# Eight gate tiles of a hybrid attention layer are computed in the recurrent stretch and applied later

## The chip, the cores and the metric

The kernel runs on one core of a Trainium2 chip. The metric is the device time of one execution in microseconds; the median of three runs is 1376.31 us (1373.77 to 1378.28). The engines are TensorE (PE, its weight loads PEld), VectorE (DVE), ScalarE (ACT), GpSimd (POOL) and SyncE (SP, which issues the DMAs here).

## The reference, cut to what matters

One layer works on 256 latent tokens, with 256 context tokens ahead of them, at width 2048. One input projection feeds two branches: an RWKV-7 recurrence (16 heads of 64) and a gated linear attention, GLA (4 heads, key 128, value 256). Each branch's output is normed and multiplied by a SiLU gate, projected to 2048, weighted by a sigmoid gate, summed and projected again.

```python
p = h @ w_in          # columns: r k v | z_a | lora_w lora_a | q_b k_b v_b | z_b | lora_g | g_a g_b
...
y_a = (y_a + bonus) * silu(z_a)
ob  = o_b * rsqrt(mean(o_b * o_b, -1) + EPS) * b_norm_g
y_b = ob.reshape(bsz, t, B_WIDTH) * silu(z_b)
mixed = sigmoid(g_a) * (y_a @ w_a) + sigmoid(g_b) * (y_b @ w_b)
return mixed @ w_out
```

Only the latent tokens need z_a, z_b, g_a and g_b. z_b has 1024 columns: eight tiles of 128 columns by 256 tokens, two for each GLA head.

## The kernel before

Weights come from HBM in fp32. A "raw" tile of 512 KB is loaded by a DMA on SP's queue (three are held, `NRAW`), and `splitter` takes it apart in two halves: ScalarE casts the half to a rounded fp32 (wH), VectorE subtracts to get the rest (wL), 128x512 elements each, up to five halves ahead (`NSPLIT`). `stream` then issues the dense matmuls, three for each block of 128 rows (high by high, high by low, low by high), into a PSUM tile "acc" (or "pv" for the values). A tile of 128 output columns over 2048 rows is 16 x 3 = 48 matmuls, of 256 columns for latent tokens alone and of 512 for all tokens (K and V). The jobs stand in one list in a fixed order (`jobs`, `pick`); a job with a `take` that says no is skipped if it has `skip`.

The instruction order of all engines is made at build time by a planner, `Issue`. Work is written as tracks (generators with a priority); `Issue.run` keeps a modelled time of each engine and picks the next step: the ready one with the lowest priority number within a short window. The dense stream has priority 99, the last. It goes ahead of other TensorE work only if 1200 ns of small work have been issued since the last dense block (`since`), or if `cooling` says that the count of matmul columns is too low. `cooling` counts columns in fixed slots of modelled time. `small` sums the modelled TensorE time of the small work.

The stages:

- the opening, up to 145 us: modulation, norm, the first seven K tiles;
- the GLA stretch (A), up to about 580 us: for each head its q, k and v columns, two K/V tiles for the recurrence (each followed by a 3x3 convolution on VectorE, `conv_ops`), and two z_b tiles (`add_zb`). `sz_track` turns a z_b tile into a gate (tanh on ScalarE, a multiply on VectorE); `gla_track` transposes the head's normed output, multiplies it by the norm's gain and the gate on VectorE, and stores it to `yb` in DRAM;
- the recurrent stretch (B), up to about 1172 us: eight pairs of heads. For each pair `fe_track` makes features, `ab_track`, `gg_track` the matrices of each chunk, `inv_track` inverts triangular blocks with 60 dependent GpSimd operations on M and tm (the "solve") and some transposes on VectorE (Lin), and `sc_track` runs the scan of 8 steps. The dense jobs r (`rc_track`), z_a (`sz_track`) and the 32 tiles of the merge gates g_a, g_b (`tg_track`, stored to DRAM) are filler. The gate jobs are let in by `pace`: job n when n <= 17 + 32 x small / 230e3;
- the merge (C): `y_track` splits the GLA branch's output, loaded from `yb` into the unused half of mB, then come w_b, w_a and w_out.

S_sz counts the two buffers of the "sz" ring, S_tg those of the "tg" ring. "C" is set in DONE when the last pair's matrices and features are made; the w_b jobs wait for it.

Of the kernel before, what the change touches and what calls it, by code (L numbers as in the profile page):

```python
# [7 lines left out]
F32 = mybir.dt.float32  # L8
# [4 lines left out]
OP = mybir.AluOpType  # L13
# [4 lines left out]
P = 128  # L18
# [6 lines left out]
class Op:  # L25


    __slots__ = ("key", "name", "call", "out", "ins", "cost", "table", "acc", "pe")

    def __init__(self, key, name, call, out, ins, func, acc, psum):  # L30
# [8 lines left out]
        if key == "pe":  # L39
# [3 lines left out]
            if name == "transpose":  # L43
# [4 lines left out]
                       n * (2 if two else 1) * ins[0].shape[0] / 128)  # L48
            c = self.pe[0] * max(self.pe[1:3])
# [27 lines left out]
class Issue:  # L77
# [10 lines left out]
    TICK, COLUMNS = 10240 / 3, 3060  # L88

    def __init__(self, ps, groups):  # L90
# [9 lines left out]
        self.corners, self.ticks = [], {}  # L100

# [37 lines left out]
    def cooling(self):  # L139

        t = self.t["pe"]
        k = int(t // self.TICK)
        rate = (2.4 if self.warm() else 1.2) * 0.6
        return 3100 - self.ticks.get(k, 0) > ((k + 1) * self.TICK - t) * rate

    def emit(self, op):
        r = op.call()
        s = max(self.t[op.key], self.start([op]) + (1220 if op.key == "dma" else 0))
        if op.key == "pe":
# [12 lines left out]
            for _ in range(n):  # L162
# [3 lines left out]
                self.ticks[int(e // self.TICK)] = self.ticks.get(int(e // self.TICK), 0) + cols  # L166
            s = e - op.cost
# [87 lines left out]
    def run(self, done):  # L255
        while not done():
# [9 lines left out]
            if best is None:  # L266
# [8 lines left out]
                if tr[6] == "pe" and best[0] != 99 and 0.6 and self.cooling():  # L275
                    best = next((x for w, x in c if x[0] == 99 and w <= w0 + 150), best)
# [54 lines left out]
def hybrid_layer(tc, a, out):  # L331
    nc = tc.nc
    es = ExitStack()
    with es:
# [197 lines left out]
        PACE0, WB = 17, 230e3  # L532
# [213 lines left out]
        yb = dp.tile([P, 8, 256], F32, name="yb")  # L746
        kv = [[dp.tile([P, 512], F32, name=f"kv{i}_{j}") for j in range(2)] for i in range(8)]
# [42 lines left out]

        def sz_track(acc, key):

            if key[0] == "b":
                yield S_sz.has()
                S_sz.n -= 1
# [43 lines left out]
        def gla_track(h, gp):  # L839
# [106 lines left out]
            for j in range(2):  # L946
                yield lambda: ("b", 2 * h + j) in szs
                pT = yield Claim("gg", [P, 2, P], "pT", *ons)
                yield [PE.transpose(pT[:, tt, :], ons[tt][:, j * P:j * P + P], ident) for tt in range(2)]
                sz = szs.pop(("b", 2 * h + j))  # L950
                yield DV.scalar_tensor_tensor(sz, pT.rearrange("p a b -> p (a b)"), bnh[:, j:j + 1], sz,
                                              op0=OP.mult, op1=OP.mult)
                rel(pT)
                yield DM.dma_start(yb[:, 2 * h + j, :], sz)
# [516 lines left out]
        def add_zb(i):  # L1471
            add_cm(w_in, C_ZB + P * i, "l", CTX, 12, lambda acc: sz_track(acc, ("b", i)))

# [24 lines left out]
        for h in range(4):  # L1498
            for x in rest[:2]:
                add_kv(*x)  # L1500
            add_zb(2 * h)
            add_zb(2 * h + 1)
# [21 lines left out]
        def pace(n):  # L1524
            return lambda: "C" in DONE or n <= PACE0 + 32 * (iss.small - state.get("b0", iss.small)) / WB

        for n in range(32):
# [295 lines left out]
```

## Time and profile before

| | |
|---|---|
| median of 3 runs | 1376.31 us |
| the profiled execution | 1373.94 us |
| its span, first to last instruction | 1372.0 us |
| mean granted TensorE clock | 0.977 of 2.4 GHz |
| TensorE, VectorE, ScalarE, GpSimd busy | 93%, 70%, 52%, 40% |

The busy shares are averages over the stages named above, which have different limits. A busy TensorE is not one at its peak: matmuls are pipelined and their ends are modelled, so one that stands alone counts with its whole latency, while 256-column matmuls in a row follow each other every 0.12 us or so though each is listed with 0.28 us. The chain that ended last tells for each stage which work the next work waited for. Granted clock means the share of 2.4 GHz that TensorE was given in the stretch; there are two levels, 1.2 and 2.4 GHz.

### The profile page before, as it was taken

What the parts mean: (1) busy time and instruction counts of PE and PEld (TensorE: products, weight loads), DVE (VectorE), ACT (ScalarE), POOL (GpSimd) and SP (SyncE); (2) the same over time, 40 slices, a digit from 0 to 9 for tenths busy, and PEclk for the clock granted to TensorE, in tenths of its full rate; (3) what the DMA queues carried; (4) which work ended last, traced back from release to release, by engine and by line L of the source; (5) the groups of instructions that cost most, each with busy time, mean ns of one, the idle gap of its engine ahead of it and who ended that gap; (6) DMA issues with size and microseconds to landing.
All of it is one profiled execution on the core that took longest, in us unless ns stands there. A gap on an engine that the chain in (4) does not pass through costs nothing.

```text
span 1372.0 us, 29669 instructions
## 1 busy us (share of the span) xinstructions
PE 1273.9 (93%) x11479; PEld 1068.6 (78%) x11479; DVE 965.8 (70%) x2031; ACT 717.3 (52%) x1449; POOL 547.8 (40%) x684
## 2 busy tenths in 40 slices
PE   5999989999999999999889999798888999999997
PEld 3555579788788897998777778677777888999877
DVE  4433496875955747767887988797869765667656
ACT  5322244443434444486587577677666656445444
POOL 0000475776560000006798629854947560000002
PEclk9999999999999999999999999899989999999999
DMA  9999465465462533566633344234333545688564
GB/s 347 354 334 305 131 205 173 131 178 162 150 181 78 142 99 102 161 183 164 162 84 87 91 121 111 68 90 113 86 80 99 136 112 149 197 246 262 184 226 144
DMA packets 311185, 220.45 MB, mean 161 GB/s; under 512 B 37354, under 2 KB 286724, under 8 KB 310532
## 3 DMA queue, kind: packets, MB, share of 16 engines
q1 hardware_dynamic: 311044, 218.55, 54.9%
q8 instruction: 90, 1.47, 0.5%
q14 instruction: 51, 0.42, 0.1%
HBM read 199.76 MB, written 12.46 MB: 155 GB/s over the span
## 4 chain that ended last, share of the span: by engine, by line
PE 54%; DVE 17%; POOL 13%; ACT 6%; DMA 5%; issue 5%; SPq 0%; DVEq 0%; ACTq 0%; POOLq 0%
PE acc L304 33%; POOL M L304 6%; POOL tm L304 6%; PE pv L304 6%; DVE wL L304 5%; PE pg L304 3%; DMA raw<-in_w_out_dram 2%; ACT Lin L304 2%; DVE kvo L304 1%; PE pS L304 1%; ACT wH L304 1%; PE pout L304 1%; DVE Lin L304 1%; DVE UV L304 1%; PE pU L304 1%
## 5 line engine op out<-in xcount | busy, mean ns | idle before, releaser
L304 DVE TENSOR_TENSOR wL<-raw,wH 128x512 fp32r<-128x512 f32 x484 | 374.5, 781 | 173.9 <-ACT wH L304 168.0
L304 ACT CAST wH<-raw 128x512 fp32r<-128x512 f32 x484 | 294.6, 615 | 338.9 <-PE acc L304 213.9
L304 PE MATMUL acc<-lH,wH 128*128 128x256 f32 x896 | 286.2, 319 | 0.5 <-ACT tg L304 0.5
L304 PE MATMUL acc<-lL,wH 128*128 128x256 f32 x896 | 257.5, 287 | 0.0
L304 PE MATMUL acc<-lH,wL 128*128 128x256 f32 x896 | 257.0, 287 | 0.1
L304 POOL TENSOR_TENSOR tm<-M 64x30 f32<-64x30 f32 (+14 forms) x240 | 162.7, 678 | 85.8 <-DVE M L304 67.5
L304 PEld LDWEIGHTS acc<-lH,wH 128*128 128x128 f32 x896 | 174.9, 195 | 21.5 <-issue 4.7
L304 POOL TENSOR_TENSOR M<-M,tm 64x30 f32<-64x30 f32 (+14 forms) x240 | 173.4, 722 | 18.7
L304 PEld LDWEIGHTS acc<-lL,wH 128*128 128x128 f32 x896 | 175.6, 196 | 3.1 <-issue 1.9
L304 PEld LDWEIGHTS acc<-lH,wL 128*128 128x128 f32 x896 | 175.4, 196 | 0.3 <-DVE wL L304 0.3
L304 PE MATMUL acc<-hH,wH 128*128 128x512 f32 (+1 forms) x416 | 168.5, 405 | 1.3 <-ACT lo L304 1.3
L304 PE MATMUL acc<-hH,wL 128*128 128x512 f32 (+1 forms) x416 | 157.3, 378 | 0.0
L304 PE MATMUL acc<-hL,wH 128*128 128x512 f32 (+1 forms) x416 | 156.5, 376 | 0.1
L304 PEld LDWEIGHTS acc<-hH,wH 128*128 128x128 f32 x416 | 78.6, 189 | 38.3 <-issue 22.9
L304 POOL TENSOR_TENSOR xs<-yg,fg 128x512 f32<-128x512 f32 (+1 forms) x10 | 13.5, 1365 | 229.8 <-DVE yg L304 229.8
L304 POOL TENSOR_TENSOR gw<-gw,csl 128x512 f32<-128x512 f32 x60 | 73.3, 1222 | 64.6 <-DMA gw<-in_w_mod_dram 64.4
L304 PEld LDWEIGHTS acc<-hH,wL 128*128 128x128 f32 x416 | 78.4, 188 | 15.4 <-DVE wL L304 0.4
L304 POOL TENSOR_TENSOR ga<-ga,gw 128x512 f32<-128x512 f32 x60 | 86.9, 1448 | 4.2
L304 PEld LDWEIGHTS acc<-hL,wH 128*128 128x128 f32 x416 | 78.8, 189 | 10.6 <-DVE hL L304 0.4
L304 PE MATMUL acc<-yH,wH 128*128 128x256 f32 x256 | 72.4, 283 | 1.6 <-DVE mt L304 1.3
L304 PE MATMUL acc<-yL,wH 128*128 128x256 f32 x256 | 72.0, 281 | 0.0
L304 PE MATMUL acc<-yH,wL 128*128 128x256 f32 x256 | 72.0, 281 | 0.0
(318 smaller groups left out, 2621.5 us busy)
## 6 DMA issues: line engine op xcount, KB each, us to landing
raw<-in_w_in_dram SPq DMA_DIRECT2D x174, 512.0 KB, 4.0
wm<-in_w_mod_dram SPq DMA_DIRECT2D x64, 512.0 KB, 6.7
gw<-in_w_mod_dram SPq DMA_DIRECT2D x64, 256.0 KB, 4.1
raw<-in_w_out_dram SPq DMA_DIRECT2D x32, 512.0 KB, 4.6
raw<-in_w_b_dram SPq DMA_DIRECT2D x16, 512.0 KB, 4.0
raw<-in_w_a_dram SPq DMA_DIRECT2D x16, 512.0 KB, 4.3
kv<-kvo SPq DMA_DIRECT2D x16, 256.0 KB, 3.7
tg<-tg SPq DMA_DIRECT2D x32, 128.0 KB, 2.9
```

Of the source, the lines that this page charges most:

```text
L304: op = Op("dma" if name == "dma_start" else self.key, name, lambda: f(*a, **k), aps[0], aps[1:], func, k.get("accum_out"), any(x.tensor.na ...
```

## The change

The eight z_b jobs leave the GLA stretch and stand ahead of the merge gates in the recurrent stretch, under the same pace, whose start goes from 17 to 25 and whose slope from 32 to 40. Their gates go to DRAM (`zs`) through the "tg" ring. A head's GLA output is only scaled by the norm's gain, now on ScalarE, and stored ungated; `y_track` loads the gates beside it and multiplies (VectorE) before the split. `cooling` counts columns over the last 2500 ns of modelled time in place of fixed slots, with small matmuls weighted down. The tiles of the triangular solve are closed once "gi", "vdone" and "bv" of the last pair are there, before it was "gi" alone.

```diff
+            self.flow = n * (1.0 if min(m, ins[0].shape[0]) > 64 else 0.75 if min(m, ins[0].shape[0]) > 32 else 0.5)
...
+    SPAN, NEED = 2500.0, 3600
...
     def cooling(self):
 
         t = self.t["pe"]
-        k = int(t // self.TICK)
-        rate = (2.4 if self.warm() else 1.2) * 0.6
-        return 3100 - self.ticks.get(k, 0) > ((k + 1) * self.TICK - t) * rate
+        while self.past and self.past[0][0] < t - self.SPAN:
+            self.flow -= self.past.popleft()[1]
+        return self.flow < self.NEED
...
+                self.past.append((e, op.flow))
+                self.flow += op.flow
...
-                if tr[6] == "pe" and best[0] != 99 and 0.6 and self.cooling():
+                if tr[6] == "pe" and best[0] != 99 and self.cooling():
...
-        PACE0, WB = 17, 230e3
+        PACE0, NPACE, WB = 25, 40, 230e3
...
+        zs = [dp.tile([P, 256], F32, name=f"zs{i}") for i in range(8)]
...
+        def zs_track(acc, i):
+
+            yield S_tg.has()
+            S_tg.n -= 1
+            sz = pools["com"].tile([P, 256], F32, name="zs", tag="tg", bufs=2)
+            yield AC.activation(sz, acc, AF.Tanh, scale=0.5)
+            yield DV.scalar_tensor_tensor(sz, sz, 1.0, acc, op0=OP.add, op1=OP.mult)
+            rel(acc)
+            yield DM.dma_start(zs[i], sz)
+            S_tg.n += 1
+            DONE.add(("zs", i))
...
             for j in range(2):
-                yield lambda: ("b", 2 * h + j) in szs
+                yield S_sz.has()
+                S_sz.n -= 1
                 pT = yield Claim("gg", [P, 2, P], "pT", *ons)
                 yield [PE.transpose(pT[:, tt, :], ons[tt][:, j * P:j * P + P], ident) for tt in range(2)]
-                sz = szs.pop(("b", 2 * h + j))
-                yield DV.scalar_tensor_tensor(sz, pT.rearrange("p a b -> p (a b)"), bnh[:, j:j + 1], sz,
-                                              op0=OP.mult, op1=OP.mult)
+                ob = pools["com"].tile([P, 256], F32, name="ob", tag="sz", bufs=2)
+                yield AC.activation(ob, pT.rearrange("p a b -> p (a b)"), AF.Copy, scale=bnh[:, j:j + 1])
                 rel(pT)
-                yield DM.dma_start(yb[:, 2 * h + j, :], sz)
+                yield DM.dma_start(yb[:, 2 * h + j, :], ob)
...
-            add_zb(2 * h)
-            add_zb(2 * h + 1)
...
         def pace(n):
-            return lambda: "C" in DONE or n <= PACE0 + 32 * (iss.small - state.get("b0", iss.small)) / WB
-
+            return lambda: "C" in DONE or n <= PACE0 + NPACE * (iss.small - state.get("b0", iss.small)) / WB
+
+        for n in range(8):
+            add_cm(w_in, C_ZB + P * n, "l", CTX, 12, lambda acc, n=n: zs_track(acc, n), take=pace(n), skip=True)
         for n in range(32):
             add_cm(w_in, (C_GA, C_GB)[n % 2] + P * (n // 2), "l", CTX, 12, lambda acc, n=n: tg_track(acc, n // 2, n % 2),
-                   take=pace(n), skip=True)
+                   take=pace(n + 8), skip=True)
...
         def y_track():
             for k in range(0, 8, 2):
+                yield lambda: ("zs", k) in DONE and ("zs", k + 1) in DONE
+                z = mg["mB"][:, k:k + 2, :]
+                for x in range(2):
+                    yield DM.dma_start(z[:, x, :], zs[k + x])
+                yield DV.tensor_tensor(land[:, k:k + 2, :], land[:, k:k + 2, :], z, op=OP.mult)
                 yield from y_split(1, k, 2, land[:, k:k + 2, :])
...
-        iss.run(lambda: ("gi", 7) in DONE)
+        iss.run(lambda: all((x, 7) in DONE for x in ("gi", "vdone", "bv")))
```

## Rows read from the trace of the kernel before

**Rows 1.** Busy time, share of the span and instructions of each engine (the page).
```profile
PE 1273.9 (93%) x11479; PEld 1068.6 (78%) x11479; DVE 965.8 (70%) x2031; ACT 717.3 (52%) x1449; POOL 547.8 (40%) x684
```

**Rows 2.** Busy time of each engine by stage: stretch, its length, engines, clock, DMA.
```profile
core 0: us, PE busy (x) PEld busy (x) DVE busy (x) ACT busy (x) POOL busy (x), PEclk, DMA share, GB/s
145.00:400.00 255.00, 239.92 (x1483) 198.94 (x1483) 193.63 (x353) 102.46 (x194) 165.94 (x134) 0.99 0.56 165
400.00:580.00 180.00, 179.27 (x1214) 157.17 (x1213) 109.69 (x266) 75.10 (x153) 11.73 (x12) 1.00 0.43 119
625.00:680.00 55.00, 48.37 (x453) 45.55 (x453) 46.62 (x69) 31.53 (x53) 46.91 (x66) 0.91 0.62 159
680.00:1060.00 380.00, 341.23 (x4350) 286.72 (x4344) 315.86 (x674) 268.54 (x572) 264.16 (x381) 0.96 0.37 94
```

**Rows 3.** The chain's shares by line, in 145 to 580 and in 625 to 1172.
```profile
by line: PE acc L304 43.6%; PE pv L304 17.7%; DVE wL L304 4.9%; DVE kvo L304 4.1%; PE pS L304 4.0%; issue 3.4%; DVE ro_t L304 2.3%; PE po L304 1.9%; PE plg L304 1.7%; DMA wg<-in_w_in_dram 1.2%; PE pk L304 1.2%; DMA gw<-in_w_mod_dram 1.0%; D
by line: POOL M L304 16.2%; PE acc L304 15.1%; POOL tm L304 14.4%; issue 7.2%; ACT Lin L304 4.3%; DVE wL L304 3.6%; DVE Lin L304 2.5%; DVE UV L304 2.3%; PE pU L304 2.2%; ACT Z L304 2.2%; PE p L304 2.1%; PE pSs L304 1.9%; PE pY L304 1.8%; DV
```

**Rows 4.** Tile acc by stretch: length, PE, PEld, DVE, ACT busy (count), clock, DMA.
```profile
580.00:1172.00 592.00, 332.78 (x2134) 281.42 (x2133) 24.34 (x59) 17.25 (x44) 0.96 0.44 114
680.00:1060.00 380.00, 185.51 (x1119) 150.81 (x1119) 18.67 (x44) 9.57 (x24) 0.96 0.37 94
1121.00:1172.00 51.00, 36.00 (x247) 30.70 (x246) 0.00 (x0) 1.91 (x5) 1.00 0.50 139
625.00:1172.00 547.00, 294.40 (x1838) 245.21 (x1839) 22.82 (x54) 14.98 (x38) 0.96 0.42 108
```

**Rows 5.** Pieces of the chain in order of time: start, us, what.
```profile
427.30 2.75 PE acc L304 x12
483.92 21.79 PE pv L304 x192
1184.31 46.54 PE acc L304 x392
```

**Rows 6.** Timeline around the end of the last scan: start, us, engine, operation.
```profile
1171.57 0.42 DVE L304 TENSOR_TENSOR xc<-pY,mu 128x256 f32<-128x256 f32 x1
1174.33 0.28 PE L304 MATMUL acc<-yH,wH 128*128 128x256 f32 x1
1174.94 0.38 ACT L304 ACTIVATE tg<-acc 128x256 f32<-128x256 f32 x1
```

**Rows 7.** Tile sz: ns min/median/max, first and last start; then within 380 to 385.
```profile
L304 DVE SCALAR_TENSOR_TENSOR sz<-sz,acc x16: 399/410/420, 280.6 to 1116.6; 128x256 f32<-128x256 f32 x16
...
L304 DVE SCALAR_TENSOR_TENSOR sz<-pT,bnh,sz x2: 472/478/484, 381.5 to 382.8; 128x256 f32<-128x256 f32 x2
```

**Rows 8.** Tile wL by stretch: length, PE, PEld, DVE busy (count), clock, DMA.
```profile
410.00:555.00 145.00, 81.76 (x257) 48.59 (x257) 36.76 (x53) 1.00 0.38 106
680.00:1060.00 380.00, 107.01 (x373) 73.14 (x373) 70.80 (x92) 0.96 0.37 94
```

**Rows 9.** VectorE's timeline: the last K/V convolution and the last GLA head's output.
```profile
579.25 0.47 DVE L304 SCALAR_TENSOR_TENSOR kvo<-acc,vec,kvo 128x255 f32<-128x255 f32 x1
...
555.00 0.48 DVE L304 SCALAR_TENSOR_TENSOR sz<-pT,bnh,sz 128x256 f32<-128x256 f32 x1 [0.51 <-PE pT L304]
```

**Rows 10.** Busy time by engine, as Rows 2, in three stretches of 10 us.
```profile
830.00:840.00 10.00, 9.57 (x96) 8.23 (x94) 9.92 (x22) 8.50 (x21) 9.45 (x8) 1.00 0.32 86
1110.00:1120.00 10.00, 9.56 (x132) 8.10 (x132) 5.25 (x14) 4.65 (x14) 8.82 (x16) 1.00 0.22 56
730.00:740.00 10.00, 7.71 (x67) 5.62 (x68) 5.62 (x8) 7.31 (x12) 8.36 (x24) 0.66 0.19 53
```

**Rows 11.** Waits in 625 to 1172: us in total, times, longest us.
```profile
DVE Lin L304 <- POOL M L304: 12.7, 4, 5.1
```

**Rows 12.** Tile tg in 580 to 700: length, ACT busy (count), clock, DMA.
```profile
580.00:700.00 120.00, 3.79 (x10) 0.94 0.62 159
```

More of the change, by code (lines that the diff above doesn't have):

```diff
@@ L1 @@
+from collections import deque
 from contextlib import ExitStack
@@ L25 @@
 class Op:
-    __slots__ = ("key", "name", "call", "out", "ins", "cost", "table", "acc", "pe")
+    __slots__ = ("key", "name", "call", "out", "ins", "cost", "table", "acc", "pe", "flow")
     def __init__(self, key, name, call, out, ins, func, acc, psum):
@@ L100, in __init__ @@
         self.corners, self.ticks = [], {}
+        self.past, self.flow = deque(), 0.0
     @staticmethod
@@ L789, in rc_track @@
             rcs[p] = o
+        def zs_track(acc, i):
[8 more added lines that the diff above has]
+            DONE.add(("zs", i))
         def sz_track(acc, key):
-            if key[0] == "b":
-                yield S_sz.has()
-                S_sz.n -= 1
             sz = pools["com"].tile([P, 256], F32, name="sz", tag="sz", bufs=2)
@@ L1469, in add_kv @@
             add_cm(w_in, (C_K, C_V)[j] + P * p, "h", ALL, 20, lambda acc: kv_track(acc, p, j))
-        def add_zb(i):
-            add_cm(w_in, C_ZB + P * i, "l", CTX, 12, lambda acc: sz_track(acc, ("b", i)))
         def gate_track():
```

## The prediction

> **What bounds the kernel now.** I read the page's busy shares first, then the chain of work that ended last, then busy time by stage. The busy shares [rows 1] say little alone: TensorE at 93% is an average over three stages with different limits, and ends of matmuls are modelled. The stages [rows 2] tell them apart. In the linear attention stretch (145 to 580 us, stage A here) TensorE is busy 239.9 of 255 us and then 179.3 of 180 us at a granted clock of 0.99 to 1.00, while VectorE has slack (193.6 of 255, 109.7 of 180). The chain inside A [rows 3] is matmuls: 43.6% projection tiles ("acc") and 17.7% the values ("pv"). A is bound by dense matmul work. In the recurrent stretch (625 to 1172 us, stage B) the chain has another face, the second line of [rows 3]: 30.6% GpSimd's triangular solve (M, tm), 15.1% dense matmuls, 3.6% the weight split on VectorE (wL), the rest a long sequence of small steps of TensorE, ScalarE and VectorE. Dense tiles are filler there. After 1172 the work is dense again (stage C: the merge and the output projection).
>
> How well is B filled? Between 680 and 1060 us TensorE ran 1119 dense matmuls [rows 4]. A dense 256-column matmul takes 46.54 / 392 = 0.1187 us back to back [rows 5], so they filled 133 of 380 us, 35%. Filler was always there: the last gate tile of the merge is evacuated at 1174.94, the first w_b matmul is issued at 1174.33, and the last scan's output is centred at 1171.57 [rows 6]. So dense work trails: what B does not take, stage C does at full price.
>
> **The change part by part.**
>
> Moved: eight z_b tiles, 48 matmuls each, 384 in all. In A they cost 384 x 0.1187 = 45.6 us of TensorE. The second head's two gates were used at 381.5 and 382.8, so half of the tiles lie before 400 us and half after [rows 7]. By the busy share of each half [rows 2] this is 22.8 x 0.94 + 22.8 x 0.996 = **44.1 us off A**. Will something else be late next? Each tile also takes its VectorE work along (four splits of 0.69 us and one multiply of 0.41 us against 5.7 us of TensorE [rows 7, 8]), so VectorE's ratio in A hardly moves. A's end is set by the last K/V convolution, 579.25, not by the last head's output, 555.00 [rows 9]; with six of the eight tiles ahead of the last values and two behind, both come forward. The last head takes 555.5 - 505.7 = 50 us from its last value matmul to its output; three K/V tiles behind it, at 48 x 2.75 / 12 = 11 us, give 33 us of cover [rows 5], and the projection tiles that follow the rest. Bounds: 30 us (the last head becomes the end, with part of its chain bare) to 46 us.
>
> Added to B: the same 384 matmuls, 32 splits and 32 casts, eight tanh, eight multiplies, eight stores. The trace does not hold this load, so I bound its price per matmul. Lower end: nothing (a gain is left to the clock's term below), if it goes into TensorE's idle time (547 us less what stages show busy: 6.6 + 38.8 us idle between 625 and 1060 alone [rows 2]). Upper end: 118.7 ns, when the tiles are only deferred to C. Between them stands what dense work costs B's chain today: (15.1 + 3.6)% of 547 us = 102 us for 1838 dense matmuls [rows 3, 4], 55.7 ns each. I take this, because it is measured in the very place: **384 x 0.0557 = +21.4 us**, bounds 0 and 45.6.
>
> VectorE and GpSimd: the 32 splits take 0.69 us each where GpSimd rests and 70.80 / 92 = 0.77 us in B [rows 8]. GpSimd suffers too: in 830 to 840 us VectorE is busy 9.92 of 10 us and GpSimd gets 8 instructions done, in 1110 to 1120 us VectorE is busy 5.25 us and GpSimd does 16 [rows 10]. More splits stretch the solve, and VectorE queued behind a late solve stands still (12.7 us of such waits [rows 11]). New VectorE work in B: 32 x 0.77 + 8 x 0.41 = 27.9 us. Part of its price is in the 55.7 ns; for the stretching of GpSimd I add **+4 us**, one sixth of the 24.6 us of splits, bounds 0 and 15.
> The Trainium skill speaks against the change here ("SBUF — State Buffer", section "Who interferes with whom"): a VectorE instruction with two SBUF inputs contends with a GpSimd instruction that reads SBUF, and the loser waits for the whole instruction. The trace agrees in kind (8 against 16 instructions). By that rule in full, 32 x 0.69 = 22 us of splits, some 70% of them beside a working GpSimd (264 of 380 us), would stand as 15 us in the sum in place of 4.
>
> The planner's count: "cooling" now asks for 3600 columns (small matmuls weighted down) over the last 2500 ns of its own modelled time, where before it asked for 3100 in a fixed slot and only once too little of the slot was left. From [rows 4] dense columns come at 1119 x 256 / 380 us = 754 per us; the other 3231 matmuls of the stage [rows 2, 4] are mostly 64 columns or fewer, some 0.4 columns per ns by the new weights (an estimate from 8.5 per us at about 45). That is about 2900 in 2500 ns, below 3600: the new rule asks for dense work most of the time, up to some 40% more than now. The old rule counted the two-pass small matmuls double, and rarely asked. This edit is what lets B take the eight tiles at all: 2134 dense matmuls between 580 and 1172 [rows 4] become 2518, 18% more. It also bears on the granted clock, which fell to 0.66 in 730 to 740, where TensorE was busy 7.7 of 10 us [rows 10]. Over 625 to 1060 the mean of 0.91 and 0.96 [rows 2] is 55 x 0.18 + 380 x 0.08 = 40 us at the lower of the two levels (1.2 and 2.4 GHz). If a third of these dips goes, 13 us run at double speed; with a quarter of the chain on TensorE that is **-3 us**, bounds -10 and +5 (a dip that stems from VectorE waiting for GpSimd is one the planner did not foresee, and it stays).
>
> The pace limits (25 and 40 for 17 and 32): tile n of the merge gates was allowed at 17 before and still is (25 less the 8 in front). By 700 us only ten had been evacuated [rows 12], so this limit did not bind; nothing.
>
> The gate applied later: eight VectorE multiplies (0.48 us each [rows 7]) in A become ScalarE copies, hidden under A's matmuls; ScalarE is busy 75 of 180 us [rows 2]. At the projection's load come eight loads on SP's queue and four VectorE multiplies of 512 columns, about 0.7 us like a split; behind them on SP stand raw weight loads and the ya stores. They fall in the time of the last two scans, and w_b starts only after the last gate tile [rows 6], so **+1 us**, bounds 0 and 4. The gla output now takes its slot from the two that the z_a tiles claim too: if both are held, the last head's copy waits, and with it B's start; that is inside A's bound of 30. Each z_b tile's new store waits on SP for VectorE's multiply; behind it queue the raw loads, which run one and a half tiles ahead, so nothing. Waiting for "vdone" and "bv" besides "gi" of the last pair: both come before or with it; nothing.
>
> Sum: -44.1 + 21.4 + 4 - 3 + 1 = **-20.7 us**. The profiled execution took 1373.94 (span 1372.0 and 1.94 around it): 1353.2. The median of the runs, 1376.31, lies 2.4 above it: **1355.6**.
>
> **The rivals.**
> *Only deferred.* B takes no more dense work at its length, and the eight tiles wait behind the last scan: 44.1 off A, 45.6 on C, 1 for the gates: 1379, no change. For it: filler was never short in B, so the issue rule and not supply sets the rate, and VectorE is at 46.6 of 55 us at B's beginning [rows 2]. Against it: the rolling count asks for more. Chance 0.17.
> *VectorE and GpSimd become the price.* The 27.9 us of new VectorE work goes on B's chain whole, beside 21.4 for the matmuls and one more stall like the longest, 5.1 us [rows 11]: -44.1 + 54.4 = +10 us, 1387, slower. It decides from 44.1 / 384 = 115 ns per added matmul. For it: VectorE at 315.9 of 380 us, GpSimd at half its rate when VectorE is full [rows 2, 10]. By the Trainium skill's rule above, taken at its full 15 us with the rest of my sum, the time would be 1367, so the page alone does not make it slower. Chance 0.18.
> *All of it fits.* The tiles go into idle TensorE time and into fewer dips: -44.1 + 8 - 6 + 1 = -41 us, 1335. For it: the last scan's 51 us held 247 dense matmuls, 4.8 per us against 2.9 in the middle of B [rows 2, 4]. Against it: that scan has no solve beside it. Chance 0.15.
> *The clock count does not do what it says* (order changes, dips remain) costs 3 us and is inside the forecast.
>
> **How the numbers follow.** Forecast 0.50 (its own range 1338 to 1371), deferred 0.17, VectorE 0.18, all fits 0.15. The predicted time is the forecast's, 1355. The range 1325 to 1388 leaves out the far half of the last two rivals. About 0.3% (4 us) is what a measurement of this kernel can tell from no change. "Deferred" is spread about its 1379: 0.03 faster, 0.12 the same, 0.02 slower. So faster 0.50 + 0.15 + 0.03 = 0.68, same 0.12, slower 0.18 + 0.02 = 0.20.
>
> **What would show it.** A ends (last K/V convolution) near 536 us in place of 580 [rows 9], with TensorE still full; dense matmuls between there and the last scan's end about 18% more, at some 3.4 per us in the middle against 2.9; the solve 1 us longer per pair; B (first transpose of M to the last scan) some 25 us longer; w_b again starting within a few us of the last scan. If B is as long as now and w_b starts 45 us after the last scan, it was deferred; if B is over 44 us longer, VectorE and GpSimd took it; if the granted clock is not above 0.977, the count's part is wrong.

## The result, and the profile after

The changed kernel takes 1388.20 us (median; 1386.03 to 1390.28) against 1375.04 for the kernel before beside it: a ratio of 1.0098, 95% interval 1.0075 to 1.0121. It is 13 us slower, where 1355 was forecast, and lies just above the range's end of 1388.

The stages of the changed kernel (stretch, its length, each engine's busy time and count, clock, DMA; A in its two parts, then 55 and 380 us of B from its first M transpose, then all of B), against [rows 2]:

```profile
core 0: us, PE busy (x) PEld busy (x) DVE busy (x) ACT busy (x) POOL busy (x), PEclk, DMA share, GB/s
145.00:400.00 255.00, 240.63 (x1483) 198.47 (x1482) 185.84 (x349) 101.97 (x192) 159.67 (x131) 0.99 0.53 159
400.00:526.00 126.00, 124.15 (x766) 102.70 (x765) 85.23 (x211) 53.34 (x116) 15.36 (x15) 1.00 0.36 104
573.70:628.70 55.00, 44.93 (x361) 42.41 (x360) 46.29 (x72) 29.53 (x51) 45.54 (x64) 0.88 0.51 134
628.70:1008.70 380.00, 340.23 (x4277) 288.74 (x4276) 307.25 (x646) 259.33 (x543) 245.06 (x352) 0.95 0.38 100
573.70:1145.10 571.40, 512.85 (x6283) 440.75 (x6283) 458.18 (x943) 372.40 (x798) 352.19 (x506) 0.95 0.42 110
```

A still keeps TensorE full, and ends earlier. VectorE's timeline has A's last K/V convolution and B's first transpose (before: 579.25 [rows 9] and 626.7):

```profile
525.87 0.47 DVE L310 SCALAR_TENSOR_TENSOR kvo<-acc,vec,kvo 128x255 f32<-128x255 f32 x1
...
573.68 1.24 DVE L310 STREAM_TRANSPOSE M<-Lin 64x1024 f32<-64x1024 f32 x1 [2.26 <-ACT Lin L310]
```

The end of the last scan, the first w_b matmul and the last merge gate, on the timelines of three engines, against [rows 6]:

```profile
1145.13 0.42 DVE L310 TENSOR_TENSOR xc<-pY,mu 128x256 f32<-128x256 f32 x1
...
1187.79 0.28 PE L310 MATMUL acc<-yH,wH 128*128 128x256 f32 x1
...
1188.39 0.38 ACT L310 ACTIVATE tg<-acc 128x256 f32<-128x256 f32 x1
```

Before, w_b started 2.8 us after the last scan; now 42.7 us. What fills these 43 us stands in the chain (start, us, what) and in the rows of the tile acc (length, PE, PEld, VectorE, ScalarE, clock, DMA; against [rows 4]):

```profile
1157.00 30.85 PE acc L310 x257
```

After, from A's end on, in the middle, in B and behind it; the last line is B before:

```profile
526.00:1145.10 619.10, 353.52 (x2255) 298.43 (x2255) 31.88 (x77) 18.49 (x47) 0.96 0.44 116
628.70:1008.70 380.00, 196.25 (x1184) 159.09 (x1183) 18.55 (x44) 9.58 (x24) 0.95 0.38 100
573.70:1145.10 571.40, 314.05 (x1955) 261.52 (x1955) 24.80 (x59) 16.10 (x41) 0.95 0.42 110
1145.10:1188.40 43.30, 42.76 (x356) 42.50 (x355) 0.00 (x0) 2.67 (x8) 1.00 0.71 192
...
626.70:1171.60 544.90, 293.13 (x1830) 243.93 (x1830) 22.82 (x54) 14.98 (x38) 0.96 0.42 107
```

B holds 1955 dense matmuls in 571.4 us, 3.42 per us; before it held 1830 in 544.9 us, 3.36 per us. The rate at which B takes filler is the old one. Behind it stand 356 dense matmuls at 0.12 us each: eight merge gates' worth (the last row's eight evacuations, x8). The eight moved tiles themselves went first. By 700 us, when B was 126 us old, three merge gates were evacuated; before, ten had been by then, when B was only 73 us old [rows 12]:

```profile
L310 ACT ACTIVATE zs<-acc x8: 366/384/387, 547.2 to 624.2; 128x256 f32<-128x256 f32 x8
...
573.70:700.00 126.30, 1.13 (x3) 0.89 0.44 114
```

The ledger by stages (us; A to the last K/V convolution, front to the first M transpose, B to the last scan, left to the last gate's evacuation, then the rest of the span):

| | A | front | B | left | rest | span |
|---|---|---|---|---|---|---|
| before | 579.2 | 47.5 | 544.9 | 3.3 | 197.1 | 1372.0 |
| after | 525.9 | 47.8 | 571.4 | 43.3 | 197.5 | 1385.9 |
| difference | -53.3 | +0.3 | +26.5 | +40.0 | +0.4 | +13.9 |

So 53 us leave A, 40 come back behind the last scan, and B grows by 26.5. Of these 26.5, the 125 matmuls that B holds more explain 15 us at 0.12 us each; 11.5 us are something else. The experiments ask why B took so little, what that cost, and what the last 13 us are.

### The profile page after: what moved, and what is told of

It reads as the page before. It is cut to its first block, busy times and chain, and to the rows that moved or that the text cites. A ratio compares the mean times of both kernels' runs of the same rounds, so it can differ in the third digit from the quotient of the medians.

```text
span 1385.9 us, 29704 instructions
## 1 busy us (share of the span) xinstructions
PE 1278.6 (92%) x11479; PEld 1072.2 (77%) x11479; DVE 975.4 (70%) x2027; ACT 720.6 (52%) x1457; POOL 548.8 (40%) x684
## 4 chain that ended last, share of the span: by engine, by line
PE 54%; DVE 17%; POOL 13%; issue 6%; DMA 5%; ACT 4%; SPq 0%; DVEq 0%; ACTq 0%; POOLq 0%
PE acc L310 32%; POOL M L310 7%; PE pv L310 6%; POOL tm L310 6%; DVE wL L310 4%; PE pg L310 3%; PE pout L310 2%; DMA raw<-in_w_out_dram 2%; ACT Lin L310 2%; ACT wH L310 1%; DVE kvo L310 1%; PE pS L310 1%; DVE Lin L310 1%; PE po L310 1%; PE pab L310 1%
## 5 line engine op out<-in xcount | busy, mean ns | idle before, releaser
L310 PE MATMUL acc<-lH,wH 128*128 128x256 f32 x928 | 297.3, 320 | 3.0 <-DVE rc L310 2.8
L310 PE MATMUL acc<-lL,wH 128*128 128x256 f32 x928 | 266.2, 287 | 0.0
L310 PE MATMUL acc<-lH,wL 128*128 128x256 f32 x928 | 265.6, 286 | 0.0
L310 PEld LDWEIGHTS acc<-lH,wH 128*128 128x128 f32 x928 | 180.6, 195 | 24.0 <-issue 5.9
L310 PEld LDWEIGHTS acc<-lL,wH 128*128 128x128 f32 x928 | 181.7, 196 | 3.3 <-issue 1.9
L310 PEld LDWEIGHTS acc<-lH,wL 128*128 128x128 f32 x928 | 181.2, 195 | 0.0
L310 PE MATMUL acc<-hH,wH 128*128 128x512 f32 (+1 forms) x384 | 161.4, 420 | 1.5 <-ACT lo L310 1.5
L310 PE MATMUL acc<-hH,wL 128*128 128x512 f32 (+1 forms) x384 | 149.2, 388 | 0.0
L310 PE MATMUL acc<-hL,wH 128*128 128x512 f32 (+1 forms) x384 | 148.5, 387 | 0.0
L310 PEld LDWEIGHTS acc<-hH,wH 128*128 128x128 f32 x384 | 73.3, 191 | 39.5 <-issue 24.0
L310 PEld LDWEIGHTS acc<-hH,wL 128*128 128x128 f32 x384 | 72.9, 190 | 15.7 <-DVE wL L310 0.4
```

The costliest lines, as they stand in the source:

```text
L310: op = Op("dma" if name == "dma_start" else self.key, name, lambda: f(*a, **k), aps[0], aps[1:], func, k.get("accum_out"), any(x.tensor.na ...
```

## The experiments

**1. Which part does it: the tiles or the count?** The changed kernel with the old `cooling`, and the kernel before with the new one.

```diff
 # e1_old_count: the changed kernel, but
-        return self.flow < self.NEED
+        return 3100 - self.ticks.get(k, 0) > ((k + 1) * self.TICK - t) * rate
 # e2_new_count_alone: the kernel before, but
-        return 3100 - self.ticks.get(k, 0) > ((k + 1) * self.TICK - t) * rate
+        return self.flow < self.NEED
```

> The changed kernel with one part undone: the column count is the fixed slot of before again, all else (gate tiles in the recurrent stretch) stays. Theory 1, the tiles are only deferred and the rolling count stretches the recurrent stretch: first transpose of M to the last scan some 545 us as before (571 with the rolling count), the gate tiles behind the last scan take 45 us or more, time 1365 to 1376, no slower than the kernel before. Theory 2, VectorE's and GpSimd's new work stretches the recurrent stretch: still about 571 us and 1385 to 1392.

> The kernel before with the rolling column count alone (gate tiles stay in the linear attention stretch). Theory 1: the recurrent stretch grows from 545 us by 15 to 26 us, dense matmuls per us in it stay within 3% of 3.4, time 1385 to 1400. Theory 2: nothing, 1372 to 1380.

Measured: 1387.97 (ratio 1.0098, 1.0074 to 1.0122) and 1370.50 (0.9976, 0.9954 to 0.9997). The count changes little in the time of the moved tiles: 0.2 us here, and 2.6 in another order (experiment 7, `since` at 1250). Tile acc in B and behind it with the old count, then in B with the new count alone:

```profile
570.30:1125.00 554.70, 290.16 (x1816) 242.90 (x1817) 24.78 (x59) 14.98 (x38) 0.95 0.41 106
1125.00:1185.60 60.60, 60.06 (x500) 59.80 (x499) 0.00 (x0) 3.83 (x11) 1.00 0.74 196
```

```profile
629.90:1197.50 567.60, 315.86 (x1984) 266.03 (x1983) 24.83 (x59) 15.44 (x39) 0.95 0.43 111
```

With the old count B takes none of the moved work: 1816 dense matmuls against 1830 before, and 500 wait behind the scan. The rolling count does push work in, and B pays for it: 139 more matmuls (1955 against 1816) for 16.7 us, **120 ns each**; in the kernel before 154 more for 22.7 us, 147 ns each. Two more pairs of runs give 103 ns (177 for 18.3 us without the tiles, experiment 2) and 115 ns (150 for 17.3 us at `since` 1250). Each B is that of one execution, and the executions of a kernel lie several us apart, so none of these is good to better than some 40 ns. Back to back one takes 118.7 ns [rows 5]. A matmul that the rule forces into B costs about what it costs behind it.

**2. What do the tiles cost at either place?** The moved tiles and the gate left out altogether, with the old and the new count:

```diff
-        for n in range(8):
-            add_cm(w_in, C_ZB + P * n, "l", CTX, 12, lambda acc, n=n: zs_track(acc, n), take=pace(n), skip=True)
...
-                yield DV.tensor_tensor(land[:, k:k + 2, :], land[:, k:k + 2, :], z, op=OP.mult)
```

> Leaves out the eight z_b tiles and the GLA branch's SiLU gate altogether, with the count of before. It gives the price of the tiles: time before less this is their price in the linear attention stretch, the time of e1_old_count less this their price in the recurrent stretch. Theory 1: both prices are near 384 x 0.1187 = 45.6 us (this kernel 1322 to 1332). Theory 2: the price in the recurrent stretch is 55 us or more, that in the linear attention stretch 45.

> Leaves out the eight z_b tiles and the GLA branch's gate, with the rolling count. Theory 1: the rolling count costs as much as with the tiles, 12 to 20 us over x_none_old (1338 to 1348), and the changed kernel's tiles cost 42 to 48 us over this. Theory 2: equal to x_none_old within 4 us, the tiles cost 55 us or more.

Measured: 1334.83 (0.9712) and 1328.02 (0.9660). In A the eight tiles are worth 1374.34 - 1334.83 = 39.5 us; moved, with the old count, 1387.97 - 1334.83 = 53.1. So leaving the tiles out altogether brings less than the 44 us that A was to lose, and moved they cost a third more. These are single orders: over the orders of experiment 7 the two prices are 37 to 49 and 46 to 53 us.

**3. Which part of a tile is dear?** On the kernel without the tiles: the matmuls of the first eight merge gates issued twice (384 more matmuls, no more loads or splits), or their splits done twice (32 more casts and subtractions, no more matmuls).

```diff
 # x_dup_pe (twice is set for the first eight merge gates)
+                    if twice:
+                        yield three(ts[0], kk, False, H[:, k, :], L[:, k, :], rH[:, kk, cl], rL[:, kk, cl],
+                                    False, kk == KT - 1)
 # x_dup_split (for the first eight merge gates, as above)
+                if jb.again:
+                    yield AC.copy(H, r)
+                    yield DV.tensor_sub(L, r, H)
```

> x_none_old (no z_b tiles, no gate on the GLA branch, the count of before) with the dense matmuls of the first eight merge-gate tiles issued twice into the same sum, so those gates are wrong: 384 more matmuls, in the same blocks of three, with no weight load, split, gate or store of their own. Theory 1, the price of a tile in the recurrent stretch is TensorE's time and what is not taken stands behind the last scan: 45.6 us over x_none_old's 1334.8, so 1376 to 1384, and the time between the last scan and the last gate tile grows from 18.7 to about 60 us. Theory 2, splits and VectorE are the price: 1350 to 1362.

> x_none_old (no z_b tiles, no gate on the GLA branch, the count of before) with the cast and the subtract of the first eight merge-gate tiles issued twice: 32 more splits of 512 columns on ScalarE and VectorE, no matmul, load or store more. x_dup_pe gave 29 us for the matmuls alone, of the 53 us that the tiles cost in the recurrent stretch. Theory A, the rest is the split's work in the recurrent chain: 15 to 25 us over 1334.8, with the stretch from the first M to the last scan 15 us or more over 542.8. Theory B, the splits hide and the rest is replanning scatter or the gate's own work: under 8 us.

Measured: 1363.89 (0.9922) and 1342.03 (0.9781): **+29.1 us** for 384 matmuls, 76 ns each, and **+7.2 us** for 32 splits. The first lies between what the two theories expected. The second says nothing of splits in B: with them the planner began B 87.1 us after A's last convolution (48.6 without), did 67 splits in that front (25 without), and B then took 535.3 us (542.8 without). It is the price of the edit as a whole. The matmuls' price does not lie in B either. Tile acc and tile wL in B, without the tiles and then with matmuls issued twice:

```profile
572.00:1114.80 542.80, 279.66 (x1773) 233.49 (x1772) 22.50 (x54) 14.56 (x37) 0.95 0.41 105
...
572.00:1114.80 542.80, 168.25 (x591) 114.62 (x591) 114.42 (x148) 0.95 0.41 105
```

```profile
570.10:1092.00 521.90, 276.11 (x1709) 227.03 (x1710) 22.77 (x54) 11.58 (x29) 0.96 0.35 91
...
570.10:1092.00 521.90, 162.51 (x569) 110.52 (x570) 91.85 (x117) 0.96 0.35 91
```

With 384 more matmuls on offer B took 64 fewer, became 20.9 us shorter (31 fewer splits were done in it), and the time from the last scan to the last gate went from 18.7 to 76.3 us. More supply does not make B take more.

**4. More by force, or none at all.** The changed kernel with the count's bound at 4800, and (with the old count) no gate tile before "C".

```diff
-    SPAN, NEED = 2500.0, 3600
+    SPAN, NEED = 2500.0, 4800          # e3_need_4800
...
-            return lambda: "C" in DONE or n <= PACE0 + NPACE * (iss.small - state.get("b0", iss.small)) / WB
+            return lambda: "C" in DONE  # x_pace_shut
```

> The changed kernel with the column count's threshold at 4800 in place of 3600: more dense blocks go ahead of the recurrent work. Theory 1, a dense matmul in the recurrent stretch costs its full 0.12 us or more: the last gate tile comes before the last scan's end, the recurrent stretch grows from 571 us by what is no longer behind it (43 us) or more, time 1385 to 1410. Theory of the prediction, 56 ns per matmul: the stretch grows by 20 us alone, time 1360 to 1370.

> e1_old_count with the z_b and merge-gate tiles let in only once the last pair's features are made, so that r and z_a alone (768 matmuls) are filler until then. Theory 1, filler costs its full time everywhere: the recurrent stretch shrinks from 555 us by about 0.119 us per matmul that leaves it (some 1000, to about 435 us), and the time stays within 15 us of 1388. Theory of the prediction, most filler is hidden: the stretch stays above 490 us and the time is over 1430. The granted clock in the stretch should fall below 0.95 in both.

Measured: 1426.19 (1.0367) and 1484.12 (1.0801). At 4800 the last gate tile is evacuated at 1084.4 while the last scan ends at 1259.3: all gates and some of w_b go into B. It holds 718 more dense matmuls than the changed kernel's (2673 against 1955) and is 112.9 us longer, 157 ns each, and the kernel is 38 us slower. Without gate tiles, B by engine and tile acc in B and behind it:

```profile
566.50:1088.60 522.10, 421.17 (x5214) 344.98 (x5215) 390.75 (x851) 311.58 (x680) 313.37 (x506) 0.77 0.26 68
...
566.50:1088.60 522.10, 153.71 (x842) 124.72 (x843) 24.88 (x59) 7.00 (x17) 0.77 0.26 68
1088.60:1285.80 197.20, 196.66 (x1639) 196.41 (x1637) 1.23 (x3) 12.83 (x34) 1.00 0.79 207
```

974 fewer dense matmuls shorten B by 32.6 us against e1_old_count, 33 ns each, and 1139 more stand behind the scan at 120 ns. The average filler is cheap; the last ones are dear. The price rises with what is already in: 33 ns over the lower half, 103 to 147 at the present filling, 157 beyond it. The 33 ns are net of the clock: without the gate tiles B ran at 0.77, with them at 0.95, so part of what the first filler costs may come back as clock. How much is not shown.

**5. The other way round.** On the kernel before: eight merge gates, two with each head, computed in A; or the eight r tiles and their convolutions, stored and loaded again.

```diff
 # v_more_a
+            for n in range(2 * h, 2 * h + 2):
+                add_cm(w_in, (C_GA, C_GB)[n % 2] + P * (n // 2), "l", CTX, 12, lambda acc, n=n: tg_track(acc, n // 2, n % 2))
...
-        for n in range(32):
+        for n in range(8, 32):
 # v_r_in_a (the stores and loads are left out here)
+            for p in (2 * h, 2 * h + 1):
+                add_cm(w_in, C_R + P * p, "l", CTX, 20, lambda acc, p=p: rs_track(acc, p))
```

> The kernel before with the move made the other way: eight of the merge-gate tiles, two per head, are computed in the linear attention stretch behind the z_b tiles, the other 24 stay as filler. Theory 1, a tile costs 40 us per eight in the linear attention stretch and 42 to 53 in the recurrent one, but filler may run out before the last scan: 1360 to 1376. Theory 2, VectorE's and GpSimd's relief in the recurrent stretch: 1355 to 1365.

> The kernel before with the eight r tiles and their convolutions computed in the linear attention stretch and stored, so that the recurrent stretch loses eight tiles of filler and 8 x 8 VectorE convolution steps. Theory A, VectorE's work sets the length of the recurrent stretch: it shrinks from 545 us by 25 us or more, and the time is 1340 to 1362. Theory B, only TensorE's time counts: 1368 to 1380.

Measured: 1369.27 (0.9983, 0.9961 to 1.0005) and 1371.26 (0.9983, 0.9960 to 1.0005): no change. B became 14 us shorter in both (530.4 and 531.9), and the last gate was through 72.5 and 61.6 us before the last scan ended, so B's end ran short of filler. Eight tiles to or from A move the time little: the two stages exchange work at about one price.

**6. The gate applied late.** The late gating with the z_b tiles computed in A and stored (old count); and e1_old_count with the tanh alone as the gate, that is without the eight VectorE multiplies that make a z_b tile its SiLU. The loads and multiplies at the projection stay in both. Both also keep the changed kernel's pace and its later closing of the solve's tiles, which no run takes by itself; the kernel without the tiles (experiment 2) has these two as well.

```diff
 # e5_gate_late: z_b stays in A, in the changed kernel with the old count
+            for n in (2 * h, 2 * h + 1):
+                add_cm(w_in, C_ZB + P * n, "l", CTX, 12, lambda acc, n=n: zs_track(acc, n))
...
-        for n in range(8):
-            add_cm(w_in, C_ZB + P * n, "l", CTX, 12, lambda acc, n=n: zs_track(acc, n), take=pace(n), skip=True)
 # x_tanh_only
-            yield DV.scalar_tensor_tensor(sz, sz, 1.0, acc, op0=OP.add, op1=OP.mult)
```

> The late gating alone: the z_b tiles are computed in the linear attention stretch as before, but their gates are stored and applied at the projection's load, with the count of before. Both theories put the whole difference on where the tiles run: within 5 us of the kernel before. If the load and the multiply ahead of the projection cost, 1380 or more.

> e1_old_count with the z_b gates stored as the tanh alone (the eight VectorE multiplies by the tile are left out, so the gate is wrong). Theory A: 2 to 5 us less than 1388 (8 x 0.41 us and the PSUM bank given back earlier). Theory B, the gate's own work holds the bank and the queue: 8 us or more less.

Measured: 1390.23 (1.0138, 1.0099 to 1.0176) and 1377.90 (1.0031, 1.0008 to 1.0054). Late gating costs 15.9 us with no tile moved, where both theories had the kernel within 5 us of before. Without their eight multiplies the moved tiles cost 10.1 us less, 3 to 4 less than in the other orders of experiment 7. That kernel is the plain case of deferral: 63.5 us between the last scan and the last gate, B as long as without the tiles (542.2 against 542.8), and 3.6 us slower than before, with all loads and multiplies of the late gating in it. So the late gating has no fixed price of 16 us; where it costs, B is longer (557.3 with the tiles in A, 544.9 before).

What makes B longer? One candidate is a stall. With late gating alone, VectorE, GpSimd and TensorE around 724 us (start, us, engine, operation, idle before and its releaser):

```profile
723.78 0.40 DVE L310 SCALAR_TENSOR_TENSOR rc<-acc,vec,rc 128x189 f32<-128x189 f32 x1
735.29 2.01 DVE L310 STREAM_TRANSPOSE Lin<-M 64x1024 f32<-64x1024 f32 x1 [11.11 <-POOL M L310]
...
735.10 0.16 POOL L310 MEMSET M<- 64x32 f32 x1
...
761.20 0.24 POOL L310 TENSOR_TENSOR tm<-M 64x30 f32<-64x30 f32 x1 [23.68 <-DVE M L310]
...
737.36 0.64 PE L310 MATMUL pH<-Lin,GMo 32*32 32x32 f32 x16 [11.28 <-DVE Lin L310]
```

The transpose of the solve's result stands at the head of VectorE's queue 11.1 us before the solve is done. Behind it wait convolutions, splits and scan steps, TensorE stands still for 11.3 us, and the next solve, whose inputs come through the same queue, starts after 23.7 us (before, the longest such gap was 21.1). But the delay does not last. The transposes that start the fourth and fifth solves, first with late gating alone (B from 627.8), then before (B from 626.7):

```profile
819.12 1.24 DVE L310 STREAM_TRANSPOSE M<-Lin 64x1024 f32<-64x1024 f32 x1
895.86 1.24 DVE L310 STREAM_TRANSPOSE M<-Lin 64x1024 f32<-64x1024 f32 x1 [1.27 <-ACT Lin L310]
...
813.82 1.24 DVE L304 STREAM_TRANSPOSE M<-Lin 64x1024 f32<-64x1024 f32 x1 [1.18 <-ACT Lin L304]
862.47 1.23 DVE L304 STREAM_TRANSPOSE M<-Lin 64x1024 f32<-64x1024 f32 x1
```

The total of this wait (VectorE's Lin for GpSimd's M) in B, B's length, and the times after B's start at which the third, fourth, fifth and eighth solve start; the other orders are those of experiment 7:

| kernel | wait, us | B, us | solves 3, 4, 5, 8 start at |
|---|---|---|---|
| without the tiles | 4.6 | 542.8 | 114, 173, 254, 446 |
| bare tanh | 4.5 | 542.2 | 113, 172, 253, 445 |
| before | 12.7 | 544.9 | 104, 187, 236, 450 |
| before, other orders | 5.7; 8.5 | 540.4; 540.9 | 103, 193, 243, 445; 104, 192, 241, 443 |
| moved tiles, old count | 13.1 | 554.7 | 132, 200, 255, 449 |
| moved tiles, other orders | 13.4; 11.6 | 549.0; 553.0 | 133, 200, 255, 450; 133, 199, 266, 456 |
| late gating alone, two orders | 19.0; 20.0 | 557.3; 556.2 | 132, 191, 268, 461; 131, 191, 262, 451 |
| changed kernel, two orders | 19.9; 17.6 | 571.4; 570.3 | 124, 199, 272, 466; 123, 198, 276, 467 |
| before with the new count | 3.1 | 567.6 | 107, 202, 261, 457 |

On average the kernels with a longer B have more of the wait, but it does not set the length: the moved tiles and the kernel before differ by 0.4 us of it and by 9.8 us of B, and the new count alone has the least of it. After the 11.1 us wait the fourth solve starts at 191 us, among the kernel before's 187 to 193; that order falls behind at the fifth. The moved tiles' eighth solve starts no later than before (449 against 450), and their B loses its 10 us after that. There is no single place, and why these orders are longer stays open. The longest wait of the changed kernel is 9.5 us, where before had 5.1 [rows 11]:

```profile
DVE Lin L310 <- POOL M L310: 19.9, 4, 9.5
```

**7. Is it the order's scatter?** The planner's threshold for looking at filler (`since`) moved from 1200 to 1150 or 1250: another order of B, no work added or moved.

```diff
-                if tr[6] == "pe" and self.since > 1200:
+                if tr[6] == "pe" and self.since > 1150:   # or 1250
```

> The kernel before with one number of the planner moved: the stretch of modelled time without TensorE work after which it looks for filler is 1150 instead of 1200 (the before value). No work is added, removed or moved between the stages; only the order in which the planner writes out the recurrent stretch differs. The disputed figure: with the old count the eight tiles stood in the linear-attention stretch at 1374 and in the recurrent one at 1388, 13 us apart. Theory S (the planner's order scatters): a change of order alone moves the time by up to 10 us in either direction, so this kernel lies anywhere from 1364 to 1385 and its recurrent stretch (first M transpose to the last scan's end) anywhere from 535 to 557 against 544.9. Theory D (the price is the tiles' own): this kernel lies within 4 us of before, 1370 to 1379, and its recurrent stretch within 4 us of 545.

> The kernel before with the same number at 1250 instead of 1200: another order, the same work in the same stages. Theory S: 1364 to 1385, and a different value from the run with 1150 by 5 us or more. Theory D: 1370 to 1379, within 4 us of before and of the run with 1150.

> The kernel with the gate tiles moved and the old count (1388.0), with 1150 instead of 1200: another order of the recurrent stretch, the same work in the same stages. Theory D: 1384 to 1392, recurrent stretch 551 to 559 and some 60 us from the last scan's end to the last gate evacuation. Theory S: anywhere from 1375 to 1395, and the recurrent stretch anywhere from 542 to 562; the 10 us by which the moved tiles' recurrent stretch was longer than before's, with fewer dense matmuls in it, would then be gone in some order.

> The kernel with the gate tiles moved and the old count, with 1250 instead of 1200. Theory D: 1384 to 1392. Theory S: 1375 to 1395, and 5 us or more from the run with 1150. In both: the time from the last scan's end to the last gate evacuation stays at 45 us or more, since the order alone does not let the stretch take the eight tiles.

> The changed kernel with the planner's number at 1250 instead of 1200: another order of the recurrent stretch, the same work in the same stages. So far the order alone moved the kernel before over 1371.6, 1373.3 and 1383.3, and the moved tiles with the old count over 1381.1, 1381.7 and 1388.0, medians 8 us apart. Theory S (a price near 8 us and a scatter of 6 us on either side): 1376 to 1390, likeliest below the 1388.2 of the change as it is; from the last scan's end to the last gate evacuation 35 to 50 us. Theory D (the change costs 13 us whatever the order): 1385 to 1392.

> The kernel with late gating alone (gate tiles still computed in the linear-attention stretch, stored, and multiplied in at the projection's load; old count; 1390.2), with 1150 instead of 1200: another order, the same work. If the late gating has a price of its own, 1384 to 1393 again, recurrent stretch 553 to 560 against 540 to 545 in the three orders of before. If its 16 us were the order's scatter, it lies with the kernel before, 1368 to 1383, and the recurrent stretch at 540 to 548.

| kernel | 1150 | 1200 | 1250 |
|---|---|---|---|
| before | 1371.61 | 1373.15 to 1375.04 | 1383.34 (1.0070, 1.0049 to 1.0092) |
| moved tiles, old count | 1381.09 (1.0056) | 1387.97 (1.0098) | 1381.72 (1.0062) |
| changed kernel | | 1388.20 (1.0098) | 1384.31 (1.0075, 1.0052 to 1.0098) |
| late gating alone | 1392.42 (1.0142) | 1390.23 (1.0138) | |

The order alone moves the kernel before by 12 us, so theory S held there. Yet the changed kernel lies above each order of before (by 1 us only for the worst against the best, which is inside the noise), and late gating alone at 1390 to 1392 twice. By means over the orders (before 1376.4, moved tiles 1383.6, changed 1386.3) the change costs 10 us, and some 3 of the 13 are this order's luck; with two or three orders each, which spread over 4 to 12 us in these three kernels, both are estimates. Behind the last scan stood 61.9 and 60.5 us in the moved tiles' other orders and 41.8 in the changed kernel's: that part no order took away. One reservation: the two orders of late gating alone agree in their first three scans within 1 us (128.4, 186.7, 253.5 us after B's start; 129.2, 187.1, 254.5), so they are not two independent draws.

## Why the prediction was wrong, point by point

**The step that failed** is the price of 55.7 ns for a dense matmul in B, and with it the sentence that the new count lets B take the eight tiles. 55.7 was the chain's share of dense work divided by all dense matmuls: an average, used for 384 additional ones. Forced in, they cost 103 to 147 ns (experiment 1); not forced, they don't go in at all. Between A's end and the last scan there are 2255 dense matmuls, 5.5% more than before, where 18% more was forecast. At 0.12 us the 384 cost 46 us where 21.4 stood, 25 of the 34 us by which the sum was off. Most of the rest is the 11.5 us by which B is longer than its dense work explains; the sum had only +4 and +1 for such things. The runs show that length, but not its cause. Of the 13 us by which the kernel is slower than before, deferral by itself is worth some 3.6 (x_tanh_only); the other 10 come with the longer B.

| term | forecast | measured | from |
|---|---|---|---|
| tiles leave A | -44.1 | -53.3 at A's end; -39.5 in the time | ledger; experiment 2 |
| their matmuls | +21.4 (0 to 45.6) | 46 at 0.12 us each; +29.1 alone, with a shorter B | experiments 1, 4; x_dup_pe |
| their splits | +4 (0 to 15) | +7.2, not paid in B | x_dup_split |
| their eight multiplies | in the same +4 | +10.1; 3 to 4 against the other orders | x_tanh_only |
| gate applied later | +1 (0 to 4) | 6.8 left over; +15.9 with the tiles in A | see below; e5_gate_late |
| the count | -3 (-10 to +5) | +0.2 and +2.6; -3.8 and -6.8 without moved tiles | experiments 1, 7; 1, 2 |
| sum | -20.7 | +13.9 | whole: +13.2 |

The measured sum takes -39.5, 29.1, 7.2, 10.1, 6.8 and 0.2. The 6.8 are what is left of the 53.1 us that the moved tiles cost, so they hold the tanh and the stores too, and the sum has to come out; its single rows are runs in different orders and good to several us.

*A.* Right in kind, and the place of its end was missed (525.9 for 536): 1170 dense matmuls were done from 100 us to A's end where 1614 had been, 444 instead of 384 fewer, since some 60 of the filler now come after the last convolution. 53.3 / 444 = 0.120 us each, the price of [rows 5]. In the time those 60 come back, at 7 us. Tile acc after and before:

```profile
100.00:525.90 425.90, 267.61 (x1170) 195.85 (x1171) 67.47 (x164) 16.23 (x27) 0.99 0.51 154
...
100.00:579.25 479.25, 320.69 (x1614) 250.16 (x1614) 74.18 (x181) 19.71 (x36) 0.99 0.53 157
```

*B.* The length was forecast (25 us longer; 26.5) and came by luck: it was to hold 384 more matmuls; it holds 125 more, worth 15 us, and 11.5 us that are no dense work. The middle's rate came to 1184 / 380 = 3.1 per us, not 3.4. The solve was not stretched: tm and M are busy 336.2 us in all, 336.0 before.

*The gate applied later.* The direct costs were as small as forecast: the eight loads are issued from 1061.8 to 1078.9, the ScalarE copies take 0.476 us, front and rest of the ledger differ by 0.3 and 0.4 us, and x_tanh_only, which has all of it, has a B of 542.2. What came besides is an order in which B is longer, in each of the seven kernels with late gating and full gates (e1_old_count and the changed kernel in all their orders, late gating alone in two). The forecast looked for a stall where work is added; the starts of the solves show none in one place. That the late gating or the multiplies cause it, and not just any change of order, is not shown.

*The count and the clock.* 0.974 instead of more than 0.977: wrong, as the forecast's own test says. B's clock stayed at 0.95 to 0.96 with either count. The term was mis-added too: 13 us at the lower level take 6.5 at the upper one, and a quarter of the 6.5 saved is 1.6 us, not 3. The pace was not run by itself; the first eight tiles went in at once, and merge gates were delayed instead.

*The rivals.* "Only deferred" is the main part: its sign, w_b 45 us after the last scan, came at 42.7, and at 60.0 with the old count. Its time, 1379, is what the tiles took where B was not longer: 1377.9 (x_tanh_only). "VectorE and GpSimd become the price" named the right time (1387), but by luck: its test, B over 44 us longer, fails, and GpSimd's solve was no slower. The wait that it built on grew, to 19.9 us, longest 9.5, from 12.7 and 5.1 [rows 11], without setting B's length (experiment 6). Its row of 8 against 16 GpSimd instructions [rows 10] compares the solve's widest operations (64x228 to 64x240) with narrower ones (64x58 to 64x210), so it shows less than a halving. Single operations do show it: in the kernel before, one update that started at the end of that full stretch of VectorE took 3.81 us, and two of its kind after 1076 us took 0.708 in the mean:

```profile
839.70 3.81 POOL L304 TENSOR_TENSOR M<-M,tm 64x240 f32<-64x240 f32 x1
...
L304 POOL TENSOR_TENSOR M<-M,tm 64x240 f32<-64x240 f32 x2 | 1.4, 708 | 0.2
```

The forecast had the argument for "deferred" in hand (filler was never short, so the rule and not the supply sets the rate) and gave it 0.17, because it took the new rule's push for free capacity.

## What to carry to other kernels

Filler in a latency-bound stretch has a rising price: take the cost of *more* filler from a run with more, never from the average of what is there; where filler already trails behind the stretch, a tile moved into it comes out at its end at full price. A change of 1% in a kernel with a planned order should be read over several orders: here they spread by up to 12 us. And an engine's queue that holds a wait for a slow engine stops what is planned behind it; whether that lengthens the stretch, the starts of the next steps of its chain tell: here a wait of 11 us was made good one solve later.

## What was unexpected of the hardware

Without the gate tiles B ran at a granted clock of 0.77 (0.95 with them), and was still 32.6 us shorter. A GpSimd operation beside an unbroken row of VectorE instructions with two SBUF inputs took three times its neighbours' time (late gating alone; VectorE was in bk, k and ar from 717.96 to 720.17):

```profile
716.30 1.04 POOL L310 TENSOR_TENSOR M<-M,tm 64x238 f32<-64x238 f32 x1
717.43 3.21 POOL L310 TENSOR_TENSOR tm<-M 64x234 f32<-64x234 f32 x1
720.72 0.71 POOL L310 TENSOR_TENSOR M<-M,tm 64x234 f32<-64x234 f32 x1
```

The Trainium skill ("SBUF — State Buffer", section "Who interferes with whom") says that a VectorE instruction with two SBUF inputs contends with a GpSimd instruction that reads SBUF. This trace agrees, and the loss, some 2.2 us, is longer than any one of those VectorE instructions (0.41 to 0.68 us): GpSimd seems to have lost several turns in a row.
